# Six raw weight places, seven per split half, new prices for the planner, and column sums by transposes, in a two-block transformer kernel

## The chip, the cores and the metric

The kernel runs on one core of a Trainium2 chip. The metric is the time of one execution on the device in microseconds (us); lower is better. The program is one launch on one core, with all weights in DRAM as float32.

## The reference

A sequence of 256 tokens with 1024 features goes through two blocks of two layers each. What matters here, cut from the reference:

```python
# first block: six modulation vectors of 1024 per layer, out of c
c_act = jax.nn.silu(c)
for layer in range(DEPTH):                        # DEPTH = 2
    mod = (c_act @ ada_w[layer] + ada_b[layer])[:, None, :]
    sh_a, sc_a, gt_a, sh_m, sc_m, gt_m = jnp.split(mod, 6, axis=-1)
    h = modulate(rms_norm(x, attn_norm[layer]), sh_a, sc_a)
    ...                                           # layer 0: diff_attention, layer 1: nsa_attention
    x = x + gt_a * mix
    h = modulate(rms_norm(x, mlp_norm[layer]), sh_m, sc_m)
    x = x + gt_m * squared_relu_mlp(h, mlp_w1[layer], mlp_w2[layer])   # 1024 -> 4096 -> 1024
    if layer == N_A_LAYERS - 1:                   # shared keys and values of layer 1
        kv_mod = (c_act @ kv_ada_w + kv_ada_b)[:, None, :]
        ...
```

The second block has a latent attention (MLA), an MLP, a block attention (MoBA) and an MLP, without modulation. The product `c_act @ ada_w` has one row, but reads two matrices of 1024 x 6144 and one of 1024 x 2048 in float32: 112 loads of 512 KB.

## The kernel before

**Tokens and weights.** The 256 tokens are two blocks of 128, `b = 0` and `b = 1`, each a stream of steps; the weights of a step are loaded once for both. A product in float32 is made of three with rounded operands: each weight is split into a high part (`wh`, a copy on ScalarE) and a low part (`wl`, a difference on VectorE), the tokens likewise (`hh`/`hl`, `rh`/`rl`). `granule()` loads 512 KB of weights (128 x 1024) into a raw place `wr` by SP's queue and splits them. The places are in `SBUF_BUFS`: four of `wr`, eight of `wh`, eight of `wl`. An MLP runs its middle hidden units for both blocks at once, with the weights as the stationary operand (`both`, results in the PSUM banks `ps_s`) and the second product from `ps_y`.

**Adaptive norm.** `ada_pair()` computes 2 x 512 columns of `c_act @ ada_w`: eight loads of 512 KB into `wr`, each multiplied by a scalar per partition and added on VectorE into `acc`. The sum over the 128 partitions follows. For a gate (kind "B", results on all partitions) it is two products with a matrix of ones. For a shift or a gain (kinds "S" and "G", feature-major) it is eight matmuls with `acc` as the stationary and one column of ones as the moving operand; of such pairs there are ten, of gates four. 112 loads belong to it. They are requested along the way, in step with the first stream, and finish with the second layer's last gate.

**The order.** The kernel is traced twice. The first trace only takes the instructions down. `schedule()`, a list scheduler, then plays them through with a model of the engines: `cost()` gives the time that an instruction holds its engine, and for a transfer the time on the DMA rings, `delay()` the time to whoever waits. Each engine takes the ready instruction of lowest rank; a tile waits until a place of its tag is free. The result is a fixed order for each engine's queue, a place for each tile, and, where the model has TensorE idle for more than 500 ns, a number of fill products (the identity times itself into a free PSUM bank) for nine tenths of that time. The second trace issues the program in that order (line 1700 for the instructions, 1698 for the fills; in the changed kernel, whose comments are gone, 1696 and 1694). So the prices decide only order, places and fills: on the chip an engine takes its queue in order and waits at the head of it for what is not there.

**Names.** `ps_t` are the PSUM banks of transposes, `T` the tiles of relative bias in attention, loaded from DRAM by GpSimd's queue into two places, `gt` a gate, `tok` normalised tokens, `rstd` the factor of a norm, `c` scratch, `modS` and `modG` the shift and gain vectors, `cst` constants.

Of the kernel before, what the change touches and what calls it, by code (L numbers as in the profile page):

```python
# [10 lines left out]
F32 = mybir.dt.float32  # L11
# [80 lines left out]
# The kernel is traced twice. The first trace only takes the instructions down; a list scheduler with a model of the  # L92
# engines' costs then gives each engine its order and each tile its place, and the second trace issues them so.
ENGINES = ("tensor", "vector", "scalar", "gpsimd", "sync")
PE, DVE, ACT, POOL, SP = range(5)
SBUF_BUFS = {"wr": 4, "wh": 8, "wl": 8, "acc": 2, "rh": 3, "rl": 3, "tok": 2, "c5": 4, "T": 2, "z": 3, "pt": 2, "o": 1,
# [6 lines left out]
class Queue:  # L103
    """stands for an engine: takes its instructions down"""
# [25 lines left out]
def cost(engine, op, aps, space):  # L130
    """time an instruction holds its engine, and a transfer the DMA rings, in ns"""
    out = aps[0]
    n, rows = flat(out), out.ap[0][1]
    if op == "dma_start":
        src = aps[1]
        dram = src if space(src) == "D" else out
        run = 4 * min((m for st, m in dram.ap if st == 1), default=1)
        total = rows * n * 4
        return {SP: 450, ACT: 457, POOL: 1040}[engine], total * 0.00278 * (1 if run >= 512 else 2)
    psum = any(space(a) == "P" for a in aps[1:])  # L140
    if engine == PE:
        width = flat(aps[1])
        if op == "transpose":
            return 107.0, 0
        if aps[1].dtype == BF16:
            return max(27 * width / 128, n / 2.4), 0
        if aps[1].dtype == F32R:
            return max(107 * width / 128, n / 2.4 + 2.5), 0
        return max(214 * width / 128, n / 0.6), 0
# [24 lines left out]
def delay(u, v, udma, vdma):  # L174
    """from the end of an instruction to the start of one that waits for it, in ns"""
# [13 lines left out]
def accesses(engine, op, args, kw):  # L189
    """the operands in memory, results first"""  # L190
# [8 lines left out]
def schedule(ops, tiles):  # L199
    """order of the instructions, slot of each tile, and where the tensor engine is kept at work; tiles: name -> (tag or  # L200
    None, space)"""
# [6 lines left out]
    for i, (engine, op, args, kw, _) in enumerate(ops):  # L208
# [16 lines left out]
        for name, box, write, sp in mine:  # L225
            for other, j, wrote in history.get(name, ()):
                # a bank of psum serves one engine at a time
# [12 lines left out]
    # transposes come before the large products that could run as well  # L240
# [8 lines left out]
    # the most tiles of a tag alive at once in the order of the trace; the slots beyond may be taken out of turn  # L249
# [53 lines left out]
    while done < n:  # L303
        again = True
        while again:
            again = False
            for e in range(5):
# [40 lines left out]
                if dma:  # L348
                    rings = end = max(end + 650, rings) + ring[i]
# [26 lines left out]
    # the tensor engine's clock halves when it rests: where it would, it gets matmuls into a free slot of psum  # L376
# [26 lines left out]
class Kernel:  # L403
# [10 lines left out]
    def later(self, n):  # L414
        """a lower priority, by n instructions, for what is taken down inside"""
# [27 lines left out]
    def weight(self, key, w, c0, n, k0, a):  # L443
        """columns c0:c0+n of the rows (k0..k0+a)*128 of w, split; one load for both token blocks"""
# [7 lines left out]
    def linear(self, name, ps, hT, w, c0, n, K, part=None):  # L452
        """ps[:, :n] = tokens @ w[:, c0:c0+n], or the part of it from the given k-tiles; yields after each granule"""
# [13 lines left out]
    def transposes(self, src, n, width=P, rev=False):  # L467
        """src [P, n, width] -> psum [width, n, P], the last in reverse if rev"""
# [11 lines left out]
    def hT(self, b):  # L480
        """the place of the normalised tokens of block b, feature-major: hi and lo"""
# [7 lines left out]
    def tsplit(self, src, nk, G=None, SH=None, scalar=None, dst=None, part=None):  # L489
        """token-major src [P, nk, 128] -> feature-major hi, lo [P, nk, 128]"""  # L490
# [25 lines left out]
    def rstd(self, ss, n, inv, eps=EPS):  # L516
        """(ss * inv + eps) ** -0.5; inv: one number, or one for each half"""
# [10 lines left out]
    def norm_T(self, b, G, SH=None):  # L528
        """rms norm of x [P, 1024] (times G plus SH) -> split, feature-major"""
        return self.tsplit(self.norm(b), KD, G, SH, dst=self.hT(b))  # L530

    def norm(self, b):
        """rms norm of x [P, 1024]"""
# [8 lines left out]
    def full_rstd(self, x, junk):  # L542
        """(mean of squares + eps) ** -0.5 of x [P, 1024]"""
# [10 lines left out]
    def raw_T(self, b, G, square=False):  # L554
        """x [P, 1024] times G -> split, feature-major; the mean of squares + eps of x, and its power -0.5 (or -1)"""
# [1147 lines left out]
```

## Time and profile before

| | |
|---|---|
| median of three runs | 1349.5 us (1347.83 to 1356.29) |
| span of the profiled execution | 1344.5 us |
| fastest run less the span | 3.3 us |
| median less the span | 5.0 us |
| TensorE, matmuls | 1301.4 us busy (97%), 8045 instructions |
| VectorE | 923.0 us (69%), 1811 |
| ScalarE | 772.9 us (57%), 1568 |
| GpSimd | 85.9 us (6%), 104 |
| moved by DMA | 273.75 MB, mean 204 GB/s |
| mean granted clock of TensorE | 0.991 |

The profile has no figure of its own for what lies around the profiled execution's span; the two differences above bound it. Times in the rows below are microseconds from the start of the span, unless a column says ns. Engines: PE is TensorE's matmuls, PEld its weight loads, DVE VectorE, ACT ScalarE, POOL GpSimd, SP the queue that issues loads. Matmuls are pipelined and their ends are modelled, so a duration of one is longer than the distance to the next; the price of a run of matmuls is read from start to start. A matmul on unrounded float32 shows as two records.

### The profile page before, as it was taken

The numbers are of one execution on the slowest core, as the hardware profiler recorded it, in microseconds if no ns is written. First come the engines' busy times: TensorE is split into PE (matmuls) and PEld (weight loads), VectorE is DVE, ScalarE is ACT, GpSimd is POOL, SyncE is SP. The second block draws the span as 40 slices with busy tenths as digits, with TensorE's granted clock in tenths as the row PEclk, the third lists the DMA queues.
The fourth block names the chain that finished last, engine by engine and source line by source line (L and its number), as shares of the span: only waits on it lengthen the run. The fifth ranks groups of instructions, "written<-read, shape, count | busy, mean of one in ns | idle before, by whom it ended". The sixth has DMA issues, their size and how long they took to land.

```text
span 1344.5 us, 21897 instructions
## 1 busy us (share of the span) xinstructions
PE 1301.4 (97%) x8045; PEld 1121.7 (83%) x8045; DVE 923.0 (69%) x1811; ACT 772.9 (57%) x1568; POOL 85.9 (6%) x104
## 2 busy tenths in 40 slices
PE   7999899999879999999999999999999999999998
PEld 6767689997768878789989887789898788899997
DVE  5777786667786788987556699575555666665552
ACT  2576675444553667766444797765444566664441
POOL 1021200000000011100000023000000111000000
PEclk9999999999889998999999999999999999999999
DMA  8888677888866744677556244475556355375551
GB/s 297 289 284 276 214 254 256 276 279 286 282 228 183 230 150 134 199 241 256 192 188 204 84 117 134 134 247 194 189 188 189 129 195 172 125 239 188 189 188 45
DMA packets 133585, 273.75 MB, mean 204 GB/s; under 512 B 25506, under 2 KB 33845, under 8 KB 133477
## 3 DMA queue, kind: packets, MB, share of 16 engines
q1 hardware_dynamic: 128533, 260.92, 59.0%
q0 software_dynamic: 3296, 10.19, 2.8%
q8 instruction: 63, 1.03, 0.3%
q10 hardware_dynamic: 1648, 1.25, 0.3%
q14 instruction: 45, 0.37, 0.1%
HBM read 269.67 MB, written 2.65 MB: 203 GB/s over the span
## 4 chain that ended last, share of the span: by engine, by line
PE 66%; DMA 2%; DVE 2%; ACT 1%; issue 0%; POOL 0%; DVEq 0%; ACTq 0%
PE ps_y L1700 35%; PE ps_s L1700 24%; PE ps_t L1700 6%; DMA wr<-in_ada_w_dram 1%; DMA wr<-in_mlp_w_dram 1%; DVE wl L1700 0%; ACT wh L1700 0%; DMA wr<-in_w_kv_dram 0%; PE ps_y L1698 0%; DVE tok L1700 0%; DVE acc L1700 0%; POOL rstd L1700 0%; ACT c L1700 0%; DVE V L1700 0%; PE ps_t L1698 0%
## 5 line engine op out<-in xcount | busy, mean ns | idle before, releaser
L1700 DVE TENSOR_TENSOR wl<-wr,wh 128x512 fp32r<-128x512 f32 (+3 forms) x536 | 464.0, 883 | 235.0 <-ACT wh L1700 228.1
L1700 ACT ACTIVATE wh<-wr 128x512 fp32r<-128x512 f32 (+3 forms) x536 | 407.6, 786 | 322.9 <-PE ps_s L1700 88.4
L1700 PE MATMUL ps_s<-hh,wh 128*128 128x256 f32 x896 | 254.5, 284 | 4.5 <-ACT c L1700 4.5
L1700 PE MATMUL ps_y<-wh,rh 128*128 128x512 f32 x640 | 255.9, 400 | 0.2 <-ACT rh L1700 0.2
L1700 PE MATMUL ps_y<-wh,rl 128*128 128x512 f32 x640 | 253.0, 397 | 2.6 <-DVE rl L1700 2.6
L1700 PE MATMUL ps_s<-hh,wl 128*128 128x256 f32 x896 | 253.4, 283 | 0.5 <-DVE wl L1700 0.3
L1700 PE MATMUL ps_s<-hl,wh 128*128 128x256 f32 x896 | 253.8, 283 | 0.0
L1700 PE MATMUL ps_y<-wl,rh 128*128 128x512 f32 x640 | 253.8, 397 | 0.0
L1700 PEld LDWEIGHTS ps_s<-hh,wh 128*128 128x128 f32 x896 | 171.2, 191 | 6.7 <-ACT c L1700 5.5
L1700 PEld LDWEIGHTS ps_s<-hl,wh 128*128 128x128 f32 x896 | 171.1, 191 | 1.4
L1700 PEld LDWEIGHTS ps_s<-hh,wl 128*128 128x128 f32 x896 | 171.3, 191 | 1.0 <-DVE wl L1700 0.9
L1700 DVE SCALAR_TENSOR_TENSOR acc<-wr,cact,acc 128x1024 f32<-128x1024 f32 x98 | 125.4, 1280 | 38.4 <-DMA wr<-in_ada_w_dram 29.8
L1700 PEld LDWEIGHTS ps_y<-wh,rl 128*128 128x128 f32 x640 | 120.3, 188 | 30.4 <-DVE rl L1700 3.9
L1700 PE MATMUL ps_y<-wh,hh 128*128 128x512 f32 (+3 forms) x360 | 140.6, 393 | 2.3 <-ACT wh L1700 1.4
L1700 PEld LDWEIGHTS ps_y<-wh,rh 128*128 128x128 f32 x640 | 120.3, 188 | 26.0 <-issue 1.5
L1700 PEld LDWEIGHTS ps_y<-wl,rh 128*128 128x128 f32 x640 | 120.7, 189 | 24.2 <-issue 0.5
L1700 PE MATMUL ps_y<-wl,hh 128*128 128x512 f32 (+3 forms) x360 | 138.5, 386 | 0.0
L1700 PE MATMUL ps_y<-wh,hl 128*128 128x512 f32 (+2 forms) x360 | 138.4, 389 | 0.0
L1700 PEld LDWEIGHTS ps_y<-wh,hh 128*128 128x128 f32 x360 | 68.2, 190 | 14.0 <-ACT wh L1700 1.9
L1700 PEld LDWEIGHTS ps_y<-wh,hl 128*128 128x128 f32 x360 | 67.9, 189 | 12.3 <-issue 1.7
L1700 PEld LDWEIGHTS ps_y<-wl,hh 128*128 128x128 f32 x360 | 68.2, 189 | 11.5 <-issue 0.3
L1700 POOL TENSOR_TENSOR rstd<-rstd,mhalf 128x2 f32<-128x2 f32 (+2 forms) x42 | 44.6, 1062 | 424.4 <-DVE rstd L1700 403.4
(202 smaller groups left out, 1561.1 us busy)
## 6 DMA issues: line engine op xcount, KB each, us to landing
wr<-in_mlp_w_dram SPq DMA_DIRECT2D x128, 512.0 KB, 4.2
wr<-in_ada_w_dram SPq DMA_DIRECT2D x96, 512.0 KB, 5.0
wr<-in_mlp_w_in_dram SPq DMA_DIRECT2D x64, 512.0 KB, 4.5
wr<-in_mlp_w_out_dram SPq DMA_DIRECT2D x64, 512.0 KB, 4.2
wr<-in_moba_w_qkv_dram SPq DMA_DIRECT2D x24, 512.0 KB, 3.9
wr<-in_a_w_in_dram SPq DMA_DIRECT2D x20, 512.0 KB, 6.0
T<-dram POOLq DMA_DIRECT2D x36, 256.0 KB, 5.1
wr<-in_kv_ada_w_dram SPq DMA_DIRECT2D x16, 512.0 KB, 6.5
```

What stands on the lines that cost most here:

```text
L1700: getattr(engines[engine], op)(*a, **k)
```

## The change

Four edits, all in numbers but the last. The comments and doc strings are removed as well; that changes only line numbers.

```diff
-SBUF_BUFS = {"wr": 4, "wh": 8, "wl": 8, "acc": 2, ...
+SBUF_BUFS = {"wr": 6, "wh": 7, "wl": 7, "acc": 2, ...
 ...
 def cost(engine, op, aps, space):
-        return {SP: 450, ACT: 457, POOL: 1040}[engine], total * 0.00278 * (1 if run >= 512 else 2)
+        return {SP: 450, ACT: 457, POOL: 1040}[engine], total * 0.0032 * (1 if run >= 512 else 2)
 ...
         if op == "transpose":
-            return 107.0, 0
+            return 109.0, 0
 ...
         if aps[1].dtype == F32R:
-            return max(107 * width / 128, n / 2.4 + 2.5), 0
-        return max(214 * width / 128, n / 0.6), 0
+            return max(119 * width / 128, n / 2.4 + 17), 0
+        return max(218 * width / 128, n / 0.6 + 4), 0
 ...
 def schedule(ops, tiles):
-                    rings = end = max(end + 650, rings) + ring[i]
+                    rings = end = max(end + 1800, rings) + ring[i]
 ...
 def ada_pair(self, w, bias, segs):
-        pm = self.ps("t")
-        for j, aj in cols(acc):
-            nc.tensor.matmul(pm[:, j:j + 1], aj, self.ones[:, 0:1].bitcast(F32), start=not begun, stop=True,
-                             skip_group_check=True)
-            begun = True
         for a, (key, col, half, kind, gain) in enumerate(segs):
+            pT = self.transposes(acc[:, a].rearrange("p (n t) -> p n t", t=P), 4)
             dst = self.mods[key]
             d = dst[:, 4 * half:4 * half + 4]
-            nc.vector.tensor_add(d, pm[:, 4 * a:4 * a + 4], self.row(bias[0], bias[1] + col // P, 4))
+            nc.vector.tensor_reduce(d, pT, axis=AX.X, op=OP.add)
+            nc.vector.tensor_add(d, d, self.row(bias[0], bias[1] + col // P, 4))
```

- Places: six raw, seven of each split half; together twenty, as before.
- Prices: a matmul on rounded operands with 512 moving columns costs the planner 230 ns instead of 216, one with 256 columns 124 instead of 109, a transpose 109 instead of 107; a load of 512 KB takes 1.68 us of the rings instead of 1.46, and starts 1.8 us after its issue instead of 0.65.
- Column sums: eight transposes into two `ps_t` banks instead of eight matmuls into one, and two row sums on VectorE over 128 x 512 from PSUM, ahead of the addition of the bias. TensorE's count of instructions in the program goes from 7764 to 7837, all of the difference fill products (138 before, 211 now); VectorE gains 20.

The whole order moves with it. Three places.

The first is SP's queue, which issues the loads, at the start of the program, from its fourth instruction on (`in_ada_w` is the adaptive norm's, `in_a_w_in` the first attention's weight; the first of those go to places outside `wr`). Before:

```order
L1700 DMA wr_22_83<-in_ada_w_dram 128x2x512
L1700 DMA wr_19_80<-in_ada_w_dram 128x2x512
L1700 DMA wr_20_81<-in_ada_w_dram 128x2x512
L1700 DMA gt_3_65<-in_a_w_in_dram 128x2x512
L1700 DMA wr_21_82<-in_ada_w_dram 128x2x512
L1700 DMA gt_2_64<-in_a_w_in_dram 128x2x512
L1700 DMA kL_1_63<-in_a_w_in_dram 128x2x512
L1700 DMA wr_22_83<-in_ada_w_dram 128x2x512
L1700 DMA kL_1_63<-in_a_w_in_dram 128x2x512
```

Now:

```order
L1696 DMA wr_22_83<-in_ada_w_dram 128x2x512
L1696 DMA wr_19_80<-in_ada_w_dram 128x2x512
L1696 DMA wr_20_81<-in_ada_w_dram 128x2x512
L1696 DMA wr_25_84<-in_ada_w_dram 128x2x512
L1696 DMA wr_21_82<-in_ada_w_dram 128x2x512
L1696 DMA wr_30_87<-in_ada_w_dram 128x2x512
L1696 DMA gt_3_65<-in_a_w_in_dram 128x2x512
L1696 DMA gt_2_64<-in_a_w_in_dram 128x2x512
L1696 DMA kL_1_63<-in_a_w_in_dram 128x2x512 x2
L1696 DMA wr_19_80<-in_ada_w_dram 128x2x512
```

Three more loads of the adaptive norm stand ahead of the first weights, in the two added places (25 and 30) and one used again.

The second is VectorE's queue at the end of the first MLP, where the first block's result `ps_y` is gated (`gt`), added to `x`, and normalised (`rstd`, and `tok` two rows behind it) for the keys and values. Before:

```order
L1700 TENSOR_TENSOR wl_44_99<-wr_20_81,wh_46_101 128x512 x2
L1700 SCALAR_TENSOR_TENSOR acc_18_79<-wr_21_82,cact_5_67,acc_18_79 128x1024
L1700 TENSOR_TENSOR c_0_10_72<-ps_y_40_95,gt_2_64 128x512
L1700 TENSOR_TENSOR x_14_14_75<-c_0_10_72,x_14_14_75 128x512
L1700 TENSOR_TENSOR c_0_10_72<-ps_y_45_100,gt_2_64 128x512
L1700 TENSOR_TENSOR x_14_14_75<-c_0_10_72,x_14_14_75 128x512
L1700 SCALAR_TENSOR_TENSOR acc_18_79<-wr_20_81,cact_5_67,acc_18_79 128x1024
L1700 TENSOR_SCALAR rstd_0_32_88<-ss_0_31_87 128x1
```

Now:

```order
L1696 TENSOR_TENSOR wl_113_125<-wr_19_80,wh_348_143 128x512 x2
L1696 TENSOR_TENSOR modG_598_148<-modG_598_148,vT_13_74 128x4
L1696 SCALAR_TENSOR_TENSOR acc_18_79<-wr_25_84,cact_5_67,acc_18_79 128x1024
L1696 SCALAR_TENSOR_TENSOR modG_598_148<-modG_598_148,vT_13_74 128x4
L1696 SCALAR_TENSOR_TENSOR acc_18_79<-wr_22_83,cact_5_67,acc_18_79 128x1024
L1696 TENSOR_TENSOR c_0_10_72<-ps_y_41_96,gt_2_64 128x512
L1696 TENSOR_TENSOR x_14_14_75<-c_0_10_72,x_14_14_75 128x512
L1696 TENSOR_TENSOR c_0_10_72<-ps_y_46_101,gt_2_64 128x512
L1696 TENSOR_TENSOR x_14_14_75<-c_0_10_72,x_14_14_75 128x512
L1696 SCALAR_TENSOR_TENSOR acc_18_79<-wr_19_80,cact_5_67,acc_18_79 128x1024
L1696 TENSOR_SCALAR rstd_0_33_90<-ss_0_32_89 128x1
```

The acc between the residual and `rstd` is still there. What differs is its raw place: before it was place 20, last read by the split six rows ahead of it; now it is place 19, last read by the split nine rows ahead, so that SP can issue its load earlier.

The third is TensorE's queue at the end of the first attention of the second token block (fills are the products with `cst` alone; `z`, `pt` and `o` are that attention's softmax weights, their transposes and its result). Before:

```order
L1700 MATMUL ps_y_57_110<-wh_183_134,rl_207_137 128x512
L1698 MATMUL ps_y_40_95<-cst_7_69 128x128 x2
L1700 MATMUL ps_t_27_84<-cst_7_69,o_128_123 128x128 x2
L1698 MATMUL ps_y_40_95<-cst_7_69 128x128 x4
L1700 MATMUL ps_y_45_100<-wh_119_121,rh_206_136 128x512
```

Now:

```order
L1696 MATMUL ps_y_58_110<-wh_42_97,rl_209_138 128x512
L1694 MATMUL ps_t_12_73<-cst_7_69 128x128 x25
L1696 MATMUL ps_t_12_73<-cst_7_69,z_87_121 128x128 x4
L1694 MATMUL ps_y_58_110<-cst_7_69 128x128 x4
L1696 MATMUL ps_t_12_73<-V_39_94,pt_141_134 128x128
L1696 MATMUL ps_t_12_73<-V_56_108,pt_141_134 128x128
L1696 MATMUL ps_t_12_73<-V_39_94,pt_141_134 128x128
L1696 MATMUL ps_t_12_73<-V_56_108,pt_141_134 128x128
L1694 MATMUL ps_y_58_110<-cst_7_69 128x128 x17
L1696 MATMUL ps_t_27_85<-cst_7_69,o_130_126 128x128
```

46 fill products stand in three groups between the last steps of that attention, where there were six.

## Rows read from the trace of the kernel before

**Rows 1.** The page: busy us, share of the span, instructions of each engine.

```profile
PE 1301.4 (97%) x8045; PEld 1121.7 (83%) x8045; DVE 923.0 (69%) x1811; ACT 772.9 (57%) x1568; POOL 85.9 (6%) x104
```

**Rows 2.** Three stretches: busy us (instructions) by engine, granted clock, DMA share, GB/s.

```profile
0.00:400.00 400.00, 366.00 (x2130) 312.72 (x2131) 293.83 (x467) 219.83 (x435) 32.45 (x43) 0.98 0.82 268
400.00:600.00 200.00, 196.58 (x1292) 160.83 (x1291) 160.64 (x507) 128.32 (x342) 15.40 (x21) 0.98 0.59 188
600.00:1345.00 745.00, 738.87 (x4626) 648.11 (x4624) 468.50 (x838) 424.80 (x793) 38.04 (x40) 1.00 0.53 173
```

**Rows 3.** TensorE's waits before 600 us: us in total, times, longest.

```profile
PE ps_t L1700 <- DVE tok L1700: 8.5, 3, 7.8
PE ps_t L1698 <- DMA cst<-in_constants_dram: 8.3, 1, 8.3
PE ps_s L1700 <- ACT c L1700: 4.5, 3, 2.8
PE ps_y L1700 <- DVE rl L1700: 2.6, 3, 1.2
```

**Rows 4.** VectorE in order of time: start, us, engine, instruction, count, idle before.

```profile
382.29 1.28 DVE L1700 SCALAR_TENSOR_TENSOR acc<-wr,cact,acc 128x1024 f32<-128x1024 f32 x1 [1.31 <-DMA wr<-in_ada_w_dram]
383.49 0.21 DVE L1700 TENSOR_SCALAR rstd<-ss 128x1 f32<-128x1 f32 x1
...
384.38 0.88 DVE L1700 TENSOR_SCALAR tok<-x,rstd 128x512 f32<-128x512 f32 x2
```

**Rows 5.** ScalarE in order of time, in the first MLP.

```profile
335.78 1.06 ACT L1700 ACTIVATE wh<-wr 128x1024 fp32r<-128x1024 f32 x1 [1.74 <-DMA wr<-in_mlp_w_dram]
...
337.26 0.58 ACT L1700 ACTIVATE c<-ps_s 128x512 f32<-128x512 f32 x1
```

**Rows 6.** VectorE in order of time, near the first MLP's end.

```profile
363.45 1.28 DVE L1700 SCALAR_TENSOR_TENSOR acc<-wr,cact,acc 128x1024 f32<-128x1024 f32 x1 [2.09 <-DMA wr<-in_ada_w_dram]
```

**Rows 7.** SP's queue before 400 us: what it waited for.

```profile
SPq L1700 <- DVE wl L1700: 142.6, 90, 5.7
SPq L1700 <- DVE acc L1700: 73.5, 67, 2.8
```

**Rows 8.** Loads before 400 us: count, KB each, median us to landing.

```profile
wr<-in_ada_w_dram SPq DMA_DIRECT2D x71, 512.0 KB, 5.0
...
T<-dram POOLq DMA_DIRECT2D x16, 256.0 KB, 5.8
```

**Rows 9.** One stretch of 10 us near the start.

```profile
10.00:20.00 10.00, 10.00 (x79) 10.00 (x79) 3.37 (x7) 3.83 (x11) 0.57 (x1) 1.00 1.04 391
```

**Rows 10.** Three stretches of 7 us.

```profile
337.00:344.00 7.00, 6.11 (x29) 6.11 (x30) 6.12 (x7) 3.99 (x6) 0.00 (x0) 0.51 0.90 287
...
381.00:388.00 7.00, 3.08 (x12) 2.79 (x13) 5.50 (x12) 3.62 (x10) 0.56 (x1) 0.53 0.50 167
...
514.00:521.00 7.00, 7.00 (x37) 5.92 (x38) 4.82 (x31) 3.69 (x13) 0.81 (x2) 0.54 0.56 190
```

**Rows 11.** TensorE in order of time: fills, transposes, column sums.

```profile
17.79 2.17 PE L1698 MATMUL ps_t<-cst 128*128 128x128 f32 x18
19.80 0.60 PE L1700 MATMUL ps_t<-cst,tok 128*128 128x128 f32 x4
20.24 0.94 PE L1698 MATMUL ps_t<-cst 128*128 128x128 f32 x7
...
45.24 1.84 PE L1700 MATMUL ps_t<-ones,acc 128*128 128x1 f32 x16
46.94 0.76 PE L1700 MATMUL ps_y<-wh,hl 128*128 128x512 f32 x1
```

**Rows 12.** Groups by line and shape: count, busy us, mean ns of one.

```profile
L1700 DVE TENSOR_REDUCE ss<-c 128x4 f32<-128x512 f32 x8 | 5.5, 683 | 0.6 <-ACT c L1700 0.6
```

**Rows 13.** ScalarE's waits after 600 us.

```profile
ACT wh L1700 <- PE ps_s L1700: 82.7, 61, 1.8
```

**Rows 14.** VectorE's waits in the first attention, 60 to 175 us.

```profile
DVE z L1700 <- DMA T<-dram: 4.1, 4, 2.2
```

More of the change, by code (lines that the diff above doesn't have):

```diff
@@ L95 @@
 PE, DVE, ACT, POOL, SP = range(5)
-SBUF_BUFS = {"wr": 4, "wh": 8, "wl": 8, "acc": 2, "rh": 3, "rl": 3, "tok": 2, "c5": 4, "T": 2, "z": 3, "pt": 2, "o": 1,
+SBUF_BUFS = {"wr": 6, "wh": 7, "wl": 7, "acc": 2, "rh": 3, "rl": 3, "tok": 2, "c5": 4, "T": 2, "z": 3, "pt": 2, "o": 1,
              "qT": 4, "kT": 1, "kL": 1, "V": 2, "gt": 2, "mx": 2, "st": 8, "r2": 4, "ss4": 8, "ss2": 8, "rstd1": 8,
@@ L793, in ada_pair @@
             nc.gpsimd.dma_start(start[0:1], dap(bias[0], bias[1] + c0, [[0, 1], [512, 2], [1, 512]]))
-        cols = lambda v: ((4 * a + j, v[:, a, j * P:(j + 1) * P]) for a in range(2) for j in range(4))
         first = True
-        begun = False
         for k in range(KD):
```

## The prediction

> **What bounds the kernel now.** I read the page first, then the table of stretches, then what TensorE waited for, then the queues behind each wait, and last the loads. TensorE is busy 1301.4 us of 1344.5 [rows 1], so 43.1 us of idle time is all that better order can win directly. The stretches tell where it lies [rows 2]: 34.0 us in the first 400 (400 less 366.00), 3.4 in the next 200, 6.1 in the last 745. Those last 745 us are simply matmuls back to back; there the DMA share is 0.53. In the first 400 it is 0.82, because the adaptive-norm matrices (112 loads of 512 KB) stream beside the weights. So the case is decided ahead of 600 us.
>
> In those 600 us 37.4 us are idle. 8.3 of them are the wait for the first constants [rows 3], which nothing here touches; 29.1 are left. Three of the causes listed there hold 14.9 (7.8 of the "tok" row, 4.5 of "c", 2.6 of "rl"), and in their long ones no engine was slow: the instruction that TensorE wanted stood in its engine's queue behind one that waited for a load. The longest: VectorE's acc was held for 1.31 us by an adaptive-norm load, and the rstd and tok that TensorE stood still for came only behind it [rows 4]. On ScalarE the same: a weight split that waited 1.74 us for its load, and the c that freed a PSUM bank two instructions later [rows 5]. On VectorE again an acc that waited 2.09 us just ahead of an rl [rows 6]. The written order expects loads sooner than they come.
>
> Why they come late: in the first 400 us SP's queue, which issues them, waited 142.6 us for a split and 73.5 us for an acc to be done [rows 7], that is for one of the four raw places. A load then takes 5.0 us from issue to landing [rows 8]. The planner of before counts 450 + 650 ns + 524,288 bytes x 0.00278 = 2.56 us for one on idle rings.
>
> **The change, part by part.**
>
> *Column sums.* Eight matmuls with one moving column took 1.70 us (from 45.24 to 46.94) [rows 11]; four transposes took 0.44 us (19.80 to 20.24), so eight take 0.88. Ten pairs: 17.0 less 8.8 = 8.2 us off TensorE. It is won only where TensorE doesn't wait right behind it; where it does, the time is worth nothing. Ends 3 and 8.2; I take 6, since most pairs stand between matmuls. VectorE gains 20 row sums over 512 elements, 683 ns in the nearest row [rows 12]: 13.7 us. It is busy 454.5 of the first 600 us [rows 2], so I cost them at nothing, covered by its idle 145 us; without that cover they are 13.7 us. Each pair now takes two PSUM "t" banks instead of one, for ten pairs; nothing for the same reason.
>
> *Prices.* A load is now planned as 450 + 1800 + 524,288 x 0.0032 ns = 3.93 us, 1.37 later than before and nearer to the 5.0 measured, so what waits for a load should move back behind what doesn't. The dumped order shows it only in part: ahead of the residual and the norm at the end of the first MLP one acc still stands before rstd (second place shown). *Raw places.* With six, the place of a load comes free two loads earlier: that acc's place was last read six rows ahead of it before, nine now, so it finds its data there more often. Together these two cut the load waits. Ends: nothing (order unchanged, or rings full) and 29.1 (every idle moment); I take 13, nearly the 14.9 traced, since the rest is attention's own chains.
>
> *Clock.* The granted clock falls to about half in three stretches of 7 us after the start [rows 10]: 0.51, 0.53, 0.54, that is to the 1.2 GHz level, each costing 7 x 0.49, 0.47, 0.46 = 3.4, 3.3, 3.2 us. Ahead of the first two lie the longest waits for loads (2.8 and 7.8 us) [rows 3]; in the third TensorE is busy all 7.00 us, so that one stays. Ends 0 and 6.7; I take one, 3.4.
>
> *Fill products.* The planner now sees more idle time and puts 123 instead of 52 fill products behind the first large one, 71 more. A fill is two records, 18 records take 2.01 us (17.79 to 19.80) [rows 11], so a fill takes 0.22 us and 71 take 15.8 us. They stand where it expects to wait: 29 behind the first 48 large products, 50 at the end of the second block's first attention, where before had a few. If the waits are real, fills cost nothing. Ends 0 and 15.8; I take 2, as before did idle near there.
>
> *Split halves, eight to seven places.* Nothing: in the long MLP stretches ScalarE waits 82.7 us for TensorE to free one [rows 13], so the places are full and one fewer is still several matmuls ahead. If that cover went, a split would be late by one ScalarE and one VectorE pass.
>
> *Start.* Nine adaptive-norm loads go ahead of the first weights instead of six (first place shown), so the first gains should be ready earlier; but the fifth weight load is still the 22nd large one, and the second batch of matmuls waits for it. Nothing, with 2 us either way.
>
> Sum: 1344.5 - 6 - 13 - 3.4 + 2 = 1324.1. The median of the three runs is 1349.5, 5.0 above the profiled span; I take those 5.0 us as what lies around it. **Forecast: 1329 us**, 1.5% below the median. Its own range: 1317 to 1337.
>
> **One rule against it.** In one stretch of 10 us the core moved 391 GB/s [rows 9], and only 268 over the first 400 us [rows 2], so by the rows the rings have room that four places leave unused. But a landing of 5.0 us may itself be queueing, and then six places only lengthen it. The Trainium skill, "DMA: Bandwidth & Descriptors", section "Anatomy of one DMA", gives about 2 us plus the bytes over 436 GB/s for one transfer (fitted on the other issuing path): by estimate 3.2 us for 512 KB. By that page 1.8 of the 5.0 us would be queueing, which speaks for the first rival, at its price below.
>
> **The rivals.**
>
> 1. *The rings, not the places, are the limit.* Loads land later by as much as they are issued earlier. For it: a load lands in 5.0 us though nothing else delays it, and the DMA share is 0.82. Against it: 391 GB/s, and SP's 216 us of waiting for places. Then only the column sums stay: 1349.5 - 6 + 2 = 1345.5.
>
> 2. *The fills cost.* The planner is now too dark: it fills waits that the chip does not have. For it: 71 more. Against: before idled 29 us. 1329 + 13.8 = 1343.
>
> 3. *Slower: the bias tables.* Each attention step of the first layer loads a bias tile of 256 KB by GpSimd's queue into one of two places; it lands in 5.8 us [rows 8] with up to four weight loads beside it. If that is shared bandwidth, six make it 5.8 x 6/4 = 8.7, 2.9 later. Sixteen such loads, two at a time: 8 x 2.9 = 23 us, if each is exposed. For it: VectorE already waits for the table four times, 4.1 us in all [rows 14], so the cover is used up; the plan leaves 46 fills at this very place. Against: 4.1 is little. It decides once a table lands later than the softmax before it ends. 1349.5 + 23 - 6 + 2 = 1368.5.
>
> 4. *Everything is won*: 8.2 + 29.1 + 6.7 = 44 us, 1305.5. No row shows an order that good.
>
> **How the numbers follow.** About 1% (13.5 us) is what a measurement of this kernel can tell from no change. Forecast 0.46, rival 1 0.20, rival 2 0.14, rival 3 0.10, rival 4 0.10. Faster by over 1% (below 1336): rival 4 and nine tenths or so of the forecast's range, 0.10 + 0.43 = 0.53. Within 1%: the rest of it and rivals 1 and 2, 0.37. Slower: 0.10. The range leaves out rival 3 and a part of rival 4: 1308 to 1352.
>
> **What would show it.** The row of tok in TensorE's waits ahead of 600 us falls from 8.5 to below 3 us; idle time of the first 600 us falls from 37.4 to about 24; SP's wait for splits and accs falls below 216 us and the DMA rate of the first 400 us rises above 268; one or two of the three clock drops are gone; eight transposes take the place of 1.70 us. If the loads' landing grows to 7 us and the rate stays, rival 1 is right; if fills stand where the matmul behind them had its operands long since, rival 2; if VectorE waits for T over 15 us in the first attention, rival 3. The forecast is wrong altogether if waits of the same length appear at other places of the first 400 us, since the order there has moved as a whole.

## The result, and the profile after

The changed kernel takes **1330.2 us** (median of four runs, 1328.8 to 1331.7), the kernel before 1348.7 (four runs beside it); the ratio is 0.985, 95% interval 0.982 to 0.988. The forecast was 1329. The profiled run took 1330.44 us with a span of 1328.7, so 1.7 us lie around a span, not the 5.0 that the forecast laid there. The forecast's sum for the span, 1324.1, was 4.6 us too low. The two errors cancel in the total: that it came within 1.2 us is luck.

The page of the change, engines, against [rows 1]:

```profile
PE 1307.1 (98%) x8111; PEld 1119.7 (84%) x8111; DVE 932.6 (70%) x1831; ACT 773.8 (58%) x1568; POOL 89.3 (7%) x104
```

TensorE is busy 5.7 us *longer* than before, in a span 15.8 us shorter: idle time fell from 43.1 to 21.6 us. The stretches of [rows 2] (the last one is cut at 1345 us as there, and so runs 16 us past the end of this span):

```profile
0.00:400.00 400.00, 387.02 (x2292) 330.38 (x2293) 312.82 (x501) 227.17 (x445) 32.69 (x43) 1.00 0.83 277
400.00:600.00 200.00, 196.88 (x1336) 160.89 (x1335) 165.78 (x509) 132.51 (x344) 16.24 (x21) 1.00 0.64 204
600.00:1345.00 745.00, 723.21 (x4486) 628.48 (x4484) 454.01 (x823) 414.11 (x781) 40.41 (x40) 1.00 0.51 164
```

In the first 600 us 16.1 us are idle (12.98 + 3.12), where it was 37.4. The rate of the first 400 us rose from 268 to 277 GB/s. TensorE's waits before 600 us, as in [rows 3]:

```profile
PE ps_t L1694 <- DMA cst<-in_constants_dram: 8.1, 1, 8.1
PE ps_t L1696 <- ACT o L1696: 2.2, 1, 2.2
PE ps_t L1696 <- DVE acc L1696: 1.7, 1, 1.7
PE ps_t L1696 <- DVE tok L1696: 0.9, 2, 0.6
```

The wait for tok went from 8.5 to 0.9 us; the rows "ps_s <- c" and "ps_y <- rl" are gone. The end of the first MLP on VectorE, as in [rows 4]:

```profile
376.06 1.27 DVE L1696 SCALAR_TENSOR_TENSOR acc<-wr,cact,acc 128x1024 f32<-128x1024 f32 x1
377.26 0.68 DVE L1696 TENSOR_TENSOR hl<-c,hh 128x512 fp32r<-128x512 f32 x1
377.86 0.20 DVE L1696 TENSOR_SCALAR rstd<-ss 128x1 f32<-128x1 f32 x1
...
379.71 0.88 DVE L1696 TENSOR_SCALAR tok<-x,rstd 128x512 f32<-128x512 f32 x2 [0.44 <-POOL rstd L1696]
```

An acc still stands ahead of rstd, but no bracket follows it: its load had landed. SP's queue and the loads before 400 us, as in [rows 7] and [rows 8], and the stretches of [rows 10]:

```profile
SPq L1696 <- DVE wl L1696: 148.4, 90, 6.6
SPq L1696 <- DVE acc L1696: 73.3, 59, 7.9
```

```profile
wr<-in_ada_w_dram SPq DMA_DIRECT2D x72, 512.0 KB, 5.5
wr<-in_mlp_w_dram SPq DMA_DIRECT2D x64, 512.0 KB, 5.7
...
T<-dram POOLq DMA_DIRECT2D x16, 256.0 KB, 6.1
```

```profile
337.00:344.00 7.00, 7.00 (x60) 6.96 (x59) 4.51 (x5) 3.28 (x4) 0.00 (x0) 1.00 0.97 294
381.00:388.00 7.00, 7.00 (x42) 5.92 (x40) 4.82 (x8) 5.84 (x13) 0.00 (x0) 1.00 0.64 217
514.00:521.00 7.00, 7.00 (x57) 5.49 (x56) 7.00 (x29) 5.98 (x18) 1.25 (x2) 1.00 0.76 224
```

SP still waits for places, 221.7 us against 216.1: as I read it, with more places it fills them and waits again, two loads further ahead. The landing of the adaptive norm's loads grew by 0.5 us. That of the first layer's MLP weights, which the prediction did not look at, grew by 1.0; before, it was

```profile
wr<-in_mlp_w_dram SPq DMA_DIRECT2D x64, 512.0 KB, 4.7
```

Neither grew by the 2 us of rival 1. The granted clock is 1.00 in all three stretches where it had fallen. And the end of the second block's first attention, where the plan put its fill products (TensorE in order of time):

```profile
159.19 5.74 PE L1694 MATMUL ps_t<-cst 128*128 128x128 f32 x50
164.96 0.83 PE L1696 MATMUL ps_t<-cst,z 128*128 128x128 f32 x4
165.63 1.06 PE L1694 MATMUL ps_y<-cst 128*128 128x128 f32 x8
166.52 1.12 PE L1696 MATMUL ps_t<-V,pt 128*128 128x128 f32 x8
167.47 3.96 PE L1694 MATMUL ps_y<-cst 128*128 128x128 f32 x34
173.62 0.33 PE L1696 MATMUL ps_t<-cst,o 128*128 128x128 f32 x1 [2.18 <-ACT o L1696]
```

Here "busy" is no work: fills hide what would be idle time. To see both at once I counted two things from the records of each run. The *stall* is, for each matmul, the time to the next start beyond its steady interval, where that is over 60 ns. The steady interval is 231 ns for 512 columns, 177 for 384, 150 for 320, 120 for 256 and some 110 for less; a halved clock counts as stall. The *fill* is the fill records at 0.111 us each. TensorE's stream from first to last matmul is stalls, fills and products. The stalls depend by about half a microsecond on the intervals taken.

Before, stalls and fills are 97.7 + 30.6 us of a stream of 1332.2. After, they are 72.0 + 46.8 of 1316.6. So stalls gave 25.7 us, fills took 16.2 back, and the column sums' own records gave 9.1 (160 at 112 ns, now 80 at 110). Together that would be 18.6 us, but the stream is only 15.6 shorter: 3 us the other way are spread over intervals and unexplained.

### The profile page after: what moved, and what is told of

It reads as the page before. It is cut to its first block, busy times and chain, and to the rows that moved or that the text cites. A ratio compares the mean times of both kernels' runs of the same rounds, so it can differ in the third digit from the quotient of the medians.

```text
span 1328.7 us, 22027 instructions
## 1 busy us (share of the span) xinstructions
PE 1307.1 (98%) x8111; PEld 1119.7 (84%) x8111; DVE 932.6 (70%) x1831; ACT 773.8 (58%) x1568; POOL 89.3 (7%) x104
## 4 chain that ended last, share of the span: by engine, by line
PE 64%; DVE 3%; ACT 2%; issue 1%; DMA 1%; POOL 0%; DVEq 0%; POOLq 0%; ACTq 0%
PE ps_y L1696 34%; PE ps_s L1696 24%; PE ps_t L1696 6%; ACT c L1696 1%; DVE wl L1696 1%; ACT wh L1696 0%; DMA T<-dram 0%; ACT hh L1696 0%; DVE z L1696 0%; DVE acc L1696 0%; DMA wr<-in_ada_w_dram 0%; POOL rstd L1696 0%; DVE tok L1696 0%; DVE c L1696 0%; DVE V L1696 0%
## 5 line engine op out<-in xcount | busy, mean ns | idle before, releaser
L1696 PEld LDWEIGHTS ps_y<-wl,rh 128*128 128x128 f32 x640 | 120.5, 188 | 25.1 <-issue 1.0
```

The lines of the kernel that those rows point to most:

```text
L1696: getattr(engines[engine], op)(*a, **k)
```

## Experiments

Ratios go against the kernel before run on the same chip with them (its medians were 1348.7 beside the change and 1350.9 to 1352.2 beside the others). "acc" and "split" are the waits for loads ahead of 600 us: of VectorE's acc for the two large adaptive-norm matrices (`in_ada_w`), and of ScalarE's splits for the MLP weights of the first block. "idle" is TensorE's in those 600 us. The third adaptive-norm matrix comes on top of "acc"; its waits were 8.2 us before, 22.2 with the places alone, 19.7 in the change without prices and 5.9 in the change.

| kernel | us | ratio, 95% interval | acc | split | idle | stall + fill |
|---|---|---|---|---|---|---|
| before | 1348.7 to 1352.2 | 1 | 29.5 | 63.5 | 37.4 | 97.7 + 30.6 |
| places alone | 1340.6 | 0.991 (0.988 to 0.994) | 38.2 | 42.9 | 31.5 | 89.3 + 31.1 |
| prices alone | 1357.9 | 1.005 (1.002 to 1.007) | 19.2 | 38.8 | 31.7 | 99.4 + 34.2 |
| sums alone | 1355.3 | 1.003 (1.000 to 1.006) | 29.5 | 58.2 | 37.1 | 100.1 + 38.9 |
| change without places | 1349.8 | 0.999 (0.997 to 1.001) | 18.3 | 41.9 | 21.8 | 82.3 + 52.4 |
| change without prices | 1332.8 | 0.987 (0.984 to 0.990) | 41.8 | 22.6 | 25.1 | 86.8 + 36.9 |
| change without sums | 1339.9 | 0.992 (0.989 to 0.995) | 9.0 | 0.4 | 17.5 | 73.2 + 41.5 |
| the change | 1330.2 | 0.985 (0.982 to 0.988) | 8.5 | 0.5 | 16.1 | 72.0 + 46.8 |
| change without late fills | 1333.1 | 0.986 (0.983 to 0.990) | 9.3 | none | 34.7 | 102.0 + 19.5 |
| seven per split half | 1363.9 | 1.009 (1.007 to 1.012) | 32.8 | 57.2 | 36.1 | 110.4 + 32.4 |
| the same, six raw, plan unaltered | 1320.2 | 0.978 (0.975 to 0.980) | 4.1 | 2.1 | 13.2 | 66.1 + 32.4 |
| that with the sums | 1311.3 | 0.970 (0.967 to 0.972) | 4.2 | 9.0 | 17.6 | 69.6 + 32.2 |
| change with eight raw | 1361.7 | 1.008 (1.006 to 1.010) | 10.0 | none | 44.1 | 116.4 + 30.4 |
| change without matmul prices | 1337.1 | 0.991 (0.988 to 0.994) | 6.5 | 1.2 | 36.5 | 96.8 + 28.0 |

**Each part alone.** The edits are those of the change, one at a time in the kernel before.

```diff
-SBUF_BUFS = {"wr": 4, "wh": 8, "wl": 8, ...
+SBUF_BUFS = {"wr": 6, "wh": 7, "wl": 7, ...
```

> The kernel before with the places alone: six raw, seven per split half; prices and column sums as before. Theory 1 (forecast: loads are issued two places earlier, so the instructions that wait for them no longer stand at the head of their queues): most of the 16 us of load waits and clock go already here, 1335 to 1341 us; VectorE's wait of acc for the adaptive-norm loads ahead of 600 us falls from 29.5 us to below 15 and ScalarE's wait of the splits for the MLP loads from 63.5 to below 30. Rival 1 (the rings are the limit): loads land later by as much as they are issued earlier, median landing about 7 us, those waits stay within a third, 1346 to 1350 us. Rival L (any edit reshuffles the order, and the gain is not the mechanism of any one part): a change of up to 6 us to either side with the waits for loads about as they were.

```diff
-    ... total * 0.00278 * (1 if run >= 512 else 2)
+    ... total * 0.0032 * (1 if run >= 512 else 2)
...
-                    rings = end = max(end + 650, rings) + ring[i]
+                    rings = end = max(end + 1800, rings) + ring[i]
```

(with the matmul and transpose prices of the change)

> The kernel before with the prices alone: loads planned as 450 + 1800 ns + 0.0032 ns per byte, matmuls and transposes dearer as in the change; places and column sums as before. Theory 1: the plan moves what waits for a load back, part of the 13 us of load waits goes, 1341 to 1347 us, and the wait of acc for loads falls by a quarter to a half. Rival P (it was the plan alone, and the places are idle): 1330 to 1337 us. Rival 1 (rings the limit): 1347 to 1351 us. Only 55 fill products stand behind the first large one here, against 52 before and 123 in the change, so by the rival in which fills cost nothing is lost to them here.

```diff
-            nc.tensor.matmul(pm[:, j:j + 1], aj, self.ones[:, 0:1].bitcast(F32), ...
...
+            pT = self.transposes(acc[:, a].rearrange("p (n t) -> p n t", t=P), 4)
+            nc.vector.tensor_reduce(d, pT, axis=AX.X, op=OP.add)
```

> The kernel before with the column sums alone done by eight transposes and two VectorE row sums; places and prices as before. Theory 1: TensorE has 8 us less to do and two thirds of it shows, 1341 to 1345 us, waits for loads as before. Rival V (VectorE's 13.7 us of row sums stand in a queue that others wait for): the 8 us are given back, 1347 to 1353 us, with row sums in the chains of TensorE's waits. Rival L (reshuffled order): anything within 6 us of the kernel before, with waits at other places.

The places alone won the time that theory 1 gave them, but not in its way: acc waited longer than before, and the splits' wait fell only to 42.9 us. The prices alone shortened the waits for loads, acc's by 35%, as theory 1 had it, and made the kernel *slower* by 0.5%, which no theory had. The sums alone, which take 9 us from TensorE, did not make it faster: 0.3% slower, with an interval that only just leaves out no change. What TensorE waited for ahead of 600 us in that run:

```profile
PE ps_t L1696 <- DVE acc L1696: 15.3, 5, 4.6
```

and TensorE in order of time, at the longest of the five:

```profile
255.18 0.90 PE L1696 MATMUL ps_t<-cst,acc 128*128 128x128 f32 x3 [4.63 <-DVE acc L1696]
```

The transposes stand in TensorE's queue ahead of the last acc of their eight, and products stood behind them. My reading, which no run shows by itself, is that the plan believed the eighth load to have come by then. Before, this row was 1.7. Rival V is not it: what is waited for is acc, not a row sum. Rival L (within 6 us, with waits at other places) held. The 15.3 us are not the whole account: TensorE's idle time is as before (37.1 against 37.4), since the wait for tok had fallen from 8.5 to 3.1. By the count of the table, what took the 9 us back is 2.4 us of stalls and 8.3 us of fills that this plan added.

**Each part taken out.** The reverse edits, in the changed kernel.

> The changed kernel with the places of before (four raw, eight per split half); new prices and new column sums stay. Theory A (the parts add up as measured alone: places -12, prices +6.5, sums +4 us): 10.5 us slower than before, 1358 to 1364 us. Theory S (they need each other; the transposes of a column sum stand in TensorE's queue until the last load of eight has come, and new prices put them later; but with four places the dearer plan is starved of loads): TensorE's wait for acc ahead of 600 us falls from the 15.3 us of the sums alone to below 5, but splits still wait for MLP loads, 30 to 60 us on ScalarE, and the time is 1345 to 1353 us. Theory L (order reshuffled, no mechanism of a part): any time within 6 us of 1351 us, the wait for acc anywhere.

> The changed kernel with the prices of before; six raw places, seven per split half, and new column sums stay. Theory A (parts add up): 8 us faster than before, 1341 to 1346 us. Theory S: the old plan expects a load after 2.56 us, so TensorE still stands for acc before the transposes, 8 to 15 us ahead of 600 us, and splits wait 30 to 45 us for MLP loads as with the places alone; 1342 to 1350 us. If instead the places alone bring the loads in time (theory 1), the wait for acc is below 5 us and the time 1330 to 1337 us.

> The changed kernel with the column sums of before (eight matmuls with one moving column); six raw places, seven per split half, and new prices stay. Theory A (parts add up): 6 us faster than before, 1343 to 1348 us. Theory S (places and prices together take the load waits away, and the sums then cost only their own time): the waits for loads are as small as with the whole change (splits below 5 us for MLP loads, acc below 15), and the time is the change's plus the 6 to 9 us of TensorE work, 1336 to 1340 us. Theory V (row sums on VectorE are a burden): as fast as the change or faster, 1326 to 1331 us.

The parts don't add up: theory A failed in all three. Theory S held without the places and without the sums; without the prices it missed (1342 to 1350 expected, TensorE's wait for acc 7.5 us), and theory 1 had the time. The **places** (six raw, and one fewer per split half) are worth 0.9, 1.6, 1.3 and 1.4% beside neither, the sums, the prices, and both. The **prices** as a whole are worth nothing that can be measured: with the rest in place, 1332.8 without and 1330.2 with, the intervals overlapping. The **sums** are worth 0.7% with the rest in place, and nothing alone.

One more thing stands in the table. The change without prices still waits 41.8 and 22.6 us for loads and takes 1332.8 us; the change waits 8.5 and 0.5 and takes 1330.2. So across plans the waits for loads do not tell the time.

In the run without places, the first 400 us look well:

```profile
0.00:400.00 400.00, 382.21 (x2259) 324.90 (x2260) 297.23 (x478) 215.48 (x424) 31.22 (x43) 1.00 0.81 262
```

16 us less idle than before, a mean clock of 1.00, and 1349.8 us all the same. Stalls fell by 15.4, fills rose by 21.8 (against the sums alone, where only the prices differ, 17.8 and 13.5): new prices move a wait out of the trace and into the plan, where a fill stands for it. As I read it, this is where the prices' gain went.

It shows in time also. With places and sums in, the 500th matmul with 256 or 512 columns starts at 198.2 us without prices and at 211.2 with them, 13.0 later. From the 1300th to the 2000th (336 to 582 us in the change) the order with prices needs 245.9 against 261.1 us. What they win there they have lost in the first 200 us.

**Fills.**

```diff
-            if count:
+            if count and end < 36000:
                 fill[i] = g, count
```

> The changed kernel in its own order on every engine, without the 123 fill products that stand behind the first large product (the 88 ahead of it stay). Rival 2 (fills cost: the plan fills waits that the chip does not have): up to 14 us faster, 1316 to 1322 us. Theory 1 (fills stand in waits that are there, and cost 2 us): without them TensorE idles instead, 1326 to 1331 us if the clock holds. Theory C (fills keep the clock up): one or more stretches of 7 us at the lower of the two levels come back at 3.3 us each, most likely where 96 of the 422 records lie, at 150 to 175 us, and the time is 1331 to 1342 us.

Rival 2 is refuted: without the 123 late fills the kernel is not faster; its median is 2.9 us above the change's, and the intervals overlap. The time lies in theory C's range and just above that of theory 1, which had asked that the clock hold. It did not: TensorE's idle time in the first 600 us rose to 34.7, and the clock fell where the fills had been, in 155 to 180 us; the change first, then the run without:

```profile
155.00:180.00 25.00, 22.78 (x167) 20.42 (x166) 21.21 (x43) 12.80 (x34) 4.25 (x3) 1.00 0.63 209
```

```profile
155.00:180.00 25.00, 15.03 (x63) 11.49 (x63) 21.22 (x43) 12.19 (x33) 2.44 (x3) 0.66 0.65 208
```

**The places by themselves.** Edit one: seven per split half in the kernel before. Edit two keeps that kernel's plan, made for four raw places, and lays the raw tiles into six afterwards:

```diff
-            "wr": 4, "wh": 8, "wl": 8
+            "wr": 4, "wh": 7, "wl": 7
...
+    places, seen = [0.0] * 6, set()
+    for i in order:
+        for t in used[i]:
+            if tiles[t][0] == "wr" and t not in seen:
+                seen.add(t)
+                slot[t] = min(range(6), key=lambda p: places[p])
+                places[slot[t]] = released[t]
     return order, slot, fill
```

> The kernel before with seven places per split half instead of eight, four raw places and all else as before. The prediction's term (a split place fewer costs nothing): 1347 to 1355 us beside a kernel before of about 1351 us, load waits as before (acc some 30 us, splits some 60 us for MLP loads). Rival H (ScalarE and VectorE now wait for TensorE to free a split half, and TensorE for the split): 5 us or more slower, with wh or wl in TensorE's waits.

> The kernel of the run above, with every engine's order, the fill products and the places of all other tiles kept as its plan wrote them, but the raw weight tiles laid into six places instead of four (each new tile takes the place that the plan frees first). So nothing is different but how early a load may start. Theory D (the places work directly: a load starts two tiles earlier and the instruction at the head of a queue finds its data): the waits of acc and of the splits for loads fall by half or more and the time by 6 to 12 us against the run above. Theory O (the gain of the places is in the order that the plan writes when it knows of six): under 3 us, load waits as above. Rival 1 (rings): the median landing grows from 5 to 7 us and the waits stay.

This settles what late loads cost in one order: with the same instructions in the same order on every engine (the two traces list them alike), 1363.9 becomes 1320.2 us, 43.7 less. Theory D was right, by far too low a price. VectorE's and ScalarE's waits for loads ahead of 600 us, with four places:

```profile
DVE acc L1700 <- DMA wr<-in_ada_w_dram: 32.8, 30, 3.8
```

```profile
ACT wh L1700 <- DMA wr<-in_mlp_w_dram: 57.2, 41, 4.1
```

with six:

```profile
DVE acc L1707 <- DMA wr<-in_ada_w_dram: 4.1, 6, 1.3
```

```profile
ACT wh L1707 <- DMA wr<-in_mlp_w_dram: 2.1, 2, 1.6
```

The 400 us of [rows 2], with four and with six:

```profile
0.00:400.00 400.00, 370.16 (x2121) 314.77 (x2122) 285.61 (x457) 214.15 (x421) 32.97 (x43) 0.96 0.80 262
```

```profile
0.00:400.00 400.00, 388.51 (x2312) 335.37 (x2313) 309.34 (x502) 228.64 (x449) 32.93 (x43) 1.00 0.84 281
```

Idle time is not all that late loads cost. In those first 600 us it fell by 22.9 us (36.1 to 13.2), about half of the gain. The mean granted clock of the whole run rose from 0.984 to 0.999; over a span of some 1360 us that is by estimate up to 20 us of time at full clock.

The landing, with four places and then with six:

```profile
wr<-in_ada_w_dram SPq DMA_DIRECT2D x69, 512.0 KB, 5.0
wr<-in_mlp_w_dram SPq DMA_DIRECT2D x64, 512.0 KB, 4.9
wr<-in_a_w_in_dram SPq DMA_DIRECT2D x20, 512.0 KB, 5.4
```

```profile
wr<-in_ada_w_dram SPq DMA_DIRECT2D x73, 512.0 KB, 5.3
wr<-in_mlp_w_dram SPq DMA_DIRECT2D x64, 512.0 KB, 5.6
wr<-in_a_w_in_dram SPq DMA_DIRECT2D x20, 512.0 KB, 6.8
```

Loads land 0.3 to 0.7 us later, the 20 of the first attention's weight 1.4, and the waits go all the same: rival 1 falls.

What is a place worth that the plan knows of? The run of the places alone also has seven per split half and the old prices, so it belongs beside the 1363.9 us too: its 1340.6 are 23.3 us less, where the unaltered plan won 43.7. (Against the kernel before it wins only 11, because the plan for seven per split half is 12 us slower by itself.) In the run of the places alone the plan issues loads earlier, but it also writes the acc earlier. From the records, the median time from the issue of an adaptive-norm load to its acc, loads and accs taken in order, is 6.0 us with four places, 7.2 with six that the plan knows of, and 8.7 with six that it doesn't. On the chip acc and splits still wait 38.2 and 42.9 us in the middle case. A place that the plan doesn't know of is slack; one that it knows is partly spent. That is not all: the change without sums also knows of six, hardly waits for loads (9.0 and 0.4 us), and takes 1339.9 us, with 16 us more of stalls and fills than the 1320.2 us run. Its order differs, and that part is open.

The 12 us that seven per split half cost by themselves are beyond the 5 of rival H. But TensorE's waits for wh and wl there rose only from 1.7 to 4.6 us, so most of it is not shown to be a lack of split places; another order may be the cause.

**How far it goes.**

> The changed kernel with eight raw places and six per split half (the same memory). With six raw places the waits for loads ahead of 600 us are already 8.5 us (acc) and under 2 us (splits), and the plan puts 49 fill products behind the first large one here instead of 123. If fills and stalls are both the time in which TensorE has no product to do, and more places shorten it further: 1318 to 1326 us. If six have taken all that loads can give: 1327 to 1334 us. If six per split half hold the splits up (rival H): 1335 us or more, with waits for TensorE on ScalarE and wh or wl in TensorE's waits.

> The changed kernel with only the matmul and transpose prices of before; the load prices, the places and the column sums of the change stay. The plan puts 38 fill products behind the first large one instead of 123. If prices only turn stalls into fills and back (what the runs without prices and without fills suggest): 1327 to 1335 us. If the dearer matmuls are what spreads VectorE's and ScalarE's work better: 1336 us or more, stalls up. If they only add fills that cost: 1316 to 1324 us.

> The run with the raw tiles in six places under a plan that counts four (prices of before, seven per split half), with the new column sums added: eight transposes and two row sums in place of eight one-column matmuls. Theory S (the transposes are worth their 9 us of TensorE only where the loads have come by then, as they have here): 5 to 10 us faster than that run, 1309 to 1316 us, with TensorE's wait for acc ahead of 600 us below 4 us. Rival L (adding the sums makes the plan write another order, which is worth up to 10 us by itself): 1316 to 1330 us. Rival V (the sums stand before loads that are late, as in the run with the sums alone): wait for acc over 8 us, above 1320 us.

Eight raw places with the change's prices and sums, the plan knowing of them (`"wr": 8, "wh": 6, "wl": 6`), are 31 us *slower* than six, with waits for loads as small. What TensorE waited for from 150 to 200 us there, and that stretch:

```profile
PE ps_t L1696 <- ACT o L1696: 5.2, 2, 2.8
PE ps_t L1696 <- DVE z L1696: 5.2, 3, 3.7
```

```profile
150.00:200.00 50.00, 35.39 (x126) 25.34 (x127) 32.44 (x80) 23.65 (x66) 5.95 (x8) 0.69 0.52 185
```

Its time is in rival H's range, but TensorE does not wait for wh or wl, so rival H as written isn't it: attention's own chain stands bare, with neither products nor fills beside it, and the clock falls. The same place (150 to 175 us) holds 96 fill records in the change and none without the matmul prices, where the first 600 us are 36.5 us idle. The orders with the new *load* price and six places reach the 500th large matmul at 211 to 214 us, those with the old price and six places at 196.0 to 201.5. My reading, which no run tests alone, is that with the new price too few products are left for that attention. Why eight places make it worse, I did not settle; the run changes raw places and split halves at once.

Without the matmul prices 18.8 us of fills are gone and 24.8 of stalls come, and the time is 6.9 us above the change's: the second of that run's three expectations held. So the prices' two halves may pull against each other: with places and sums in, the load price takes 1332.8 to 1337.1 us (the intervals overlap), and the matmul prices then take 1337.1 to 1330.2.

The last run adds the sums, under a plan that still counts four raw places, and theory S held: 1311.3 us, 3.0% below the kernel before and 1.4% below the change. TensorE's waits for acc are 1.7 us, as before the change:

```profile
PE ps_t L1703 <- DVE c L1703: 1.7, 1, 1.7
PE ps_t L1703 <- DVE acc L1703: 1.7, 1, 1.7
```

## Why the prediction was right, and where it was not

The time and the kind of gain were right: late loads at the head of VectorE's and ScalarE's queues held TensorE up, and the change took that away. The sizes were not. In terms of TensorE's stream, stalls gave 25.7 us where the load and clock terms had 13 + 3.4, fills took 16.2 where the sum had 2, and the column sums gave 9.1 where it had 6. The span fell by 15.8 us, not 20.4. That the time still met the forecast is in part luck, by these errors and the 5.0 us laid around the span.

**The bound: right in kind, too small in size.** The idle time was largely that of late loads, ahead of 600 us. But that idle time "is all that better order can win directly" was too small a bound. With the lateness taken away and nothing else, in the order for seven per split half, the span fell by 45.1 us (1360.6 to 1315.5) and idle time only by 23.2 (42.4 to 19.2). Late loads had cost granted clock as well.

**Load waits, -13 for prices and places together: mis-sized, and wrongly shared.** Idle time of the first 600 us fell by 21.3 us, where I expected some 13. But part of it came back as fills, which I priced at +2 and which took 16.2 us of TensorE. Set against each other as one, "time without a product", stalls and fills fell by 9.5 us, where the load, clock and fill terms together had 14.4. Of the prices I wrote that what waits for a load "should move back"; with the rest in place the waits for loads did fall, and that is no gain by itself: the runs with and without prices differ by less than the intervals.

**Extra fills, +2: near in what they cost, wrong as a term.** They fill real waits; removing them gains nothing. But they stand for time without a product, which the sum counted as won.

**Column sums, -6: right with the rest in place, wrong alone.** From the medians they are worth 0.7% of 1351, 9.5 us, with the rest in place, and 8.9 (1320.2 to 1311.3) under the plan that counts four. Both are near the 9.1 of the records and above my upper end of 8.2, though the intervals are some 4 us wide to either side. "Most pairs stand between matmuls" failed with late loads: 15.3 us of waiting. VectorE's 20 row sums (685 ns, 13.7 us) were covered, as I wrote: TensorE's wait for what they make is 0.3 us ahead of 600 us in the change.

**Clock, -3.4: too low.** All three drops went, 9.9 us by the prediction's own sum, though part of that lies in time in which TensorE waited anyway. The third went too, which I had called one that stays, since TensorE was busy through it. One of 1.7 us (28 to 35 us at 0.76) is new, as one from 47 to 54 us (0.76) is gone.

**Split halves, 0: open.** Alone, one place fewer came with 0.9%; in the change its part can't be told from the order's.

**Signs.** SP's waits were the wrong one: I read 216 us of waiting for places as a shortage, and expected less with more places. It did not fall in the change, nor in the fastest run (152.0 and 72.9 us, 224.9 together). In one and the same order it rose from 194.6 us with four places to 220.9 with six, while the time fell by 43.7.

**Rivals.** Rival 1 fell: landing grew by 0.3 to 1.4 us, the waits went, and the rate rose to 281 GB/s with six places under the same order. The prediction took 5.0 us for the landing of all loads; it is that of the adaptive norm's. The Trainium skill, "DMA: Bandwidth & Descriptors", section "Anatomy of one DMA", had spoken for rival 1: by estimate from its fit for one transfer, 3.2 us for 512 KB, so that 1.8 of the 5.0 us would be queueing. The trace does not refute that: the quickest group of such loads in the kernel before, those of the last attention's output weights, lands in 3.5 us. But two more raw places added only the 0.3 to 1.4 us.

Rival 3 fell: tables land in 6.1 us and VectorE waits 1.2 us for them in 600 us, less than before. Rival 4, 1305.5 us, had been given for want of an order that good; one at 1311.3 exists.

## What to carry to other kernels

When a planner writes a static order, try giving the chip more buffers than the plan counts. Here two raw places that the plan did not know of won 43.7 us, where a plan that knew of the same two, with the same prices, won 23.3 from the same start. Planning with slower loads and dearer matmuls is no substitute: with the rest in place it won nothing that can be measured.

Count stalls and filler work as one number, since a plan that sees more idle time turns one into the other without winning time. Don't read a load queue that waits for a free buffer as starved. Whether the engines that read wait for data tells more, but only between runs of the same order: across plans, 1332.8 us went with 64 us of such waits, and 1361.7 with 10.

## What was not expected of the hardware

Going from four to six raw places of 512 KB, in the same order, lengthened the median landing of the adaptive norm's loads only from 5.0 to 5.3 us and of the first layer's MLP weights from 4.9 to 5.6 (the 20 loads of the first attention's weight went from 5.4 to 6.8), while the mean rate of the first 400 us rose from 262 to 281 GB/s.

And filler matmuls that look like pure loss cost nothing that can be measured. Where they were taken out, the mean granted clock of 155 to 180 us was 0.66 instead of 1.00 (a large part of it at the 1.2 GHz level), and the time was not shorter.
